# Projection units in another order, their weights split without the second rounded copy, weight sums started elsewhere, norm sums copied by ScalarE

## The chip, the cores and the metric

The kernel runs on one core of a Trainium2 chip. A core has a matrix engine (TensorE, PE in the rows; PEld is its weight load), VectorE (DVE), ScalarE (ACT), GpSimd (POOL) and a queue that issues DMAs (SP). The metric is the device time of one execution in microseconds: 2397.79 us is the median of three runs of the kernel before (2397.59 to 2398.81).

## What is computed

One streaming step of a one-layer encoder trunk on 1024 prompt frames and 64 sample frames (1088 tokens, 1024 channels, all float32):

```
h = x + 1/2 * SwiGLU_1(RMSNorm(x))
z = RMSNorm(h) @ w_in            # columns [u_ssm 512 | q 512 | k 512 | v 512]
y_ssm = GLU(S5(u_ssm))           # diagonal complex state, scan over time; gelu; y * sigmoid(y @ w_glu + b)
y_att = DiffAttn(q, k, v)        # 4 heads
h = h + concat(y_ssm, y_att) @ w_out
h = h + CrossAttn(RMSNorm(h), RMSNorm(mem))      # weights w_cq, w_ck, w_cv, w_co
x = h + 1/2 * SwiGLU_2(RMSNorm(h))
y = RMSNorm(x)
```

It also returns k and v of the new tokens, the memory's k and v and the last S5 states. The change lies almost wholly in the second line, the input projection, and in what runs beside it.

## The kernel before

**Float32 by three products.** Each operand of a matmul is split into a rounded high part and the rest. `mm3` (L172) then makes three matmuls per tile, high by high, high by low and low by high. For the weights, `load_w` (L166) loads 128x512 pieces (tiles `wr`, four buffers) and `w_split` (L155) splits each into `wh` and `wl` (seven buffers each). There are two ways to split. The staged one (`split_into`, L147 to L154) has ScalarE write the high part twice, once as `wh` into SBUF (L152) and once into a PSUM bank `q` (L153), and VectorE subtract `q` from the raw weights (L154). The tag `q` has one buffer. The other way (L162, L163) has ScalarE write `wh` only and VectorE subtract `wh`.

**The projection stage.** `w_in` is done in 16 units of 128 output columns: u0 to u3, then k, q and v of each head. One unit loads two pieces of weights and runs 72 matmuls into three PSUM banks (`unit`, `units`, L179 to L193); VectorE then multiplies the banks by the token norms `rb` (L1387 for u units, L203 for the others). PSUM has seven such banks beside `q`. The rows of 1088 tokens come from one pool of 36 buffers.

**The norms.** FFN1 delivers eight rows of `h` (`mix_row`). For each, `Stats.add` squares it on ScalarE (L259) and adds it to a sum on GpSimd (L260, seven adds after the first row). When all are in, `Stats.rstd` reduces the sum over channels by matmuls with ones (L269), VectorE forms the roots (L220 to L232), PE transposes them (L138) and ScalarE writes `rb`. TensorE has the matmuls with ones right behind the 72 matmuls of the first unit, u0.

**S5.** Each u unit starts one chain `s5_main`: store u, load it regrouped, matmuls (L1291), scans on VectorE (`scaled` and `scan`, L1262 to L1272), the scan over blocks in a small tile `gs` (from L1305, with its first writes L1305 and L1308), loads, the y products on TensorE (L1340, L1341) and gelu on ScalarE (L1342), stores (L1345).

**Weight sums.** Later square layers use sums and differences of four 512x512 quarters of a weight. `weight_sums` makes them on GpSimd: for each k of four, four tiles are loaded (L478, two DMAs each), four additions run on each (L482 to L485) and the tile is stored (L486). 16 tiles and 64 additions a weight. The tiles are of the tag `ws`, four buffers, which `gs` shares. Before, `w_out` is summed beside FFN1 and `w_co`, then `w_cq`, from head 2 of the projection stage on.

**The order.** The order of instructions on each engine, and of DMAs on SP, is set once at build time by a scheduler that simulates the program; on the chip each engine and each queue then goes through its own list in order, and an instruction that waits holds up all that stand behind it on its engine. `bg` holds generators that are advanced (`pump_all`) between units.

**Normed.finish** is called twice in FFN2; it reduces norms as `Stats.rstd` does, and two small copies (L602, L603) take the result out of PSUM.

Of the kernel before, what the change touches and what calls it, by code (L numbers as in the profile page):

```python
# [17 lines left out]
P = 128  # L18
# [3 lines left out]
NS = 64  # L22
# [9 lines left out]
NC = NT // TS  # L32
NCP = NP // TS
NPAIR = 16
SUMS_AT = 2
S_CHS = ((0, 360), (360, 720), (720, 1088))
NROWS = 36
BIG = 3.0e38
# [31 lines left out]
def tile_hymba_step(ctx: ExitStack, tc: tile.TileContext, a, o):  # L70
# [24 lines left out]
    def row(shape=(P, NT), dt=F32):  # L95
        return rows.tile(list(shape), dt, tag="r", name=nm("r"))
# [13 lines left out]
    bg = deque()  # L110
# [10 lines left out]
    def pump_all():  # L121

        for g in list(bg):
            try:
                next(g)
            except StopIteration:
                bg.remove(g)
# [38 lines left out]
    def load_w(src, staged=True):  # L166

        parts = [w_split(w_raw(src[:, k:k + 4]), staged) for k in range(0, src.shape[1], 4)]
        return [(hi[:, k], lo[:, k]) for hi, lo in parts for k in range(4)]
# [9 lines left out]
    def units(wsrcs, xs, mid=None, at=None, chs=CHS):  # L179


        n = len(xs)
        ws = [load_w(src) for src in wsrcs]
        ps_ = [[bank() for _ in range(3)] for _ in ws]
        for k0, k1 in ((0, at or n), (at or n, n)):
            for w, p in zip(ws, ps_):
                mm3(p, ((*w[k], *xs[k]) for k in range(k0, k1)), n, chs, k0)
            if mid and k0 == 0:
                mid()
        return ps_  # L190
# [279 lines left out]
    def weight_sums(n, w, swap=False):  # L470

        i11, i21, i12, i22 = (1, 0, 3, 2) if swap else (0, 1, 2, 3)
        for k in range(4):
            ts = [half([P, 4, P]) for _ in range(4)]
            for c, t in enumerate(ts):
                for h in range(2):
                    wj = w[(4 * h + k) * P:(4 * h + k + 1) * P].rearrange("p (h c n) -> p h c n", h=2, c=4)
                    load(out=t[:, 2 * h:2 * h + 2], in_=wj[:, :, c])  # L478
            yield
            for c, t in enumerate(ts):  # L480
                a11, a21, a12, a22 = (t[:, i] for i in (i11, i21, i12, i22))
                G.tensor_tensor(out=a22, in0=a21, in1=a22, op=ALU.add)  # L482
                G.tensor_tensor(out=a21, in0=a11, in1=a21, op=ALU.subtract)
                G.tensor_tensor(out=a11, in0=a22, in1=a11, op=ALU.subtract)
                G.tensor_tensor(out=a12, in0=a12, in1=a11, op=ALU.subtract)  # L485
                store(out=sums_d[n, k, c], in_=t)  # L486
# [85 lines left out]
    class Normed:  # L572
# [22 lines left out]
        def finish(self, c):  # L595
            ssq = small([P, 5], "hq")
            V.memset(ssq, 1.0)
            p = bank()
            for t, (t0, n) in enumerate(HTILES):
                T.matmul(p[:n, 4 * t:4 * t + 4], self.acc[:, c, t0:t0 + n], ones[:, 0:4], start=True, stop=True)  # L600
            n = HT - 512
            V.tensor_copy(ssq[:, 0:4], p[:, 0:16].rearrange("p (t n) -> p t n", n=4)[:, :, 0])  # L602
            V.tensor_copy(ssq[:n, 4:5], p[:n, 16:17])  # L603
            if self.rb is None:
                self.rb = row()
            yield from half_rstd(ssq, self.rb, c)
# [667 lines left out]
    def s5_main(f, u):  # L1274
        js = slice(4 * f, 4 * f + 4)

        store(out=u_d[f], in_=u)
        w1 = row([P, 4, 2, P])
        load(out=w1, in_=w1_d[f])
        u8 = row([P, 8, NC])  # L1280
        for s in range(TS):
            load(out=u8[16 * s:16 * s + 16], in_=u_d[f, :, s].rearrange("(g h) c -> h g c", h=16))
        yield
        yield

        p = [bank() for _ in range(3)]
        for i in range(8):
            q, j = i // 4, i % 4
            e = p[i // 3][:, (i % 3) * NC:(i % 3 + 1) * NC]
            for r in range(2):  # L1290
                T.matmul(e[64 * r:64 * r + 64], w1[:, j, q, 64 * r:64 * r + 64], u8[:, 2 * j + r],  # L1291
                         start=True, stop=True)
        x = row([P, 8, NC])
        three(x, p)
        yield

        r_ = row()
        tu = r_[:, 0:544], r_[:, 544:1088]
        for k in (1, 2, 4):
            scan(x, k, tu, f, (apr, api, apn))  # L1300
            yield

        gs = half([P, 152]).rearrange("p (r n) -> p r n", n=19)
        xe = x.rearrange("p r (s i) -> p r s i", i=8)[:, :, :, 7]
        V.memset(gs[:, :, 0:1], 0.0)  # L1305
        V.tensor_copy(gs[:, :, 1:17], xe[:, :, 0:16])
        for q in range(2):
            V.tensor_copy(gs[:, 4 * q:4 * q + 4, 17], cf[:, 6 + q, js])  # L1308
        V.tensor_tensor(out=gs[:, :, 18:19], in0=xe[:, :, 16:17],
                        in1=scaled(tu, f, (apr, api, apn), 7, 1, gs[:, :, 17:18], 1)[:, :, :, 0], op=ALU.add)  # L1310
        for k in (1, 2, 4, 8):
            scan(gs[:, :, 1:17], k, tu, f, wide)
        for b in range(2):
            for q in range(2):
                V.tensor_copy(s_fin[:, b, q, js], gs[:, 4 * q:4 * q + 4, 16 + 2 * b])
        V.tensor_copy(gs[:, :, 16:17], gs[:, :, 17:18])
        yield
        s_ = row([P, 8, NC])
        sv, xv = (z.rearrange("p r (s i) -> p r s i", i=8) for z in (s_, x))
        V.tensor_copy(sv[:, :, :, 0], gs[:, :, 0:17])  # L1320
        scaled((sv[:, :, :, 1:8], row()), f, (apr, api, apn), 0, 7, gs[:, :, 0:17], 17)
        V.tensor_tensor(out=sv[:, :, :, 1:8], in0=xv[:, :, :, 0:7], in1=sv[:, :, :, 1:8], op=ALU.add)
        yield
        xs_ = row([P, 8, NC])
        for i in range(2):
            for q in range(2):
                load(out=xs_[64 * i:64 * i + 64, q::2], in_=s_[64 * q:64 * q + 64, 4 * i:4 * i + 4])
        yield
        m, rk = row([P, 8, P]), row([P, 8, P])
        load(out=m, in_=m_d[f])  # L1330
        load(out=rk, in_=rk_d[f].rearrange("p g s h -> p g (s h)"))
        yield
        yield

        y8 = s_
        for b, n in ((0, 3), (1, 3), (2, 2)):
            p = bank()
            for g in range(n):
                q = p[:, g * NC:(g + 1) * NC]
                T.matmul(q, m[:, 3 * b + g], u8[:, 3 * b + g], start=True, stop=False)  # L1340
                T.matmul(q, rk[:, 3 * b + g], xs_[:, 3 * b + g], start=False, stop=True)  # L1341
            A.activation(y8[:, 3 * b:3 * b + n].rearrange("p g n -> p (g n)"), p[:, :n * NC], AF.Gelu_apprx_tanh)  # L1342
            yield
        for s in range(TS):
            store(out=ys_d[f, :, s].rearrange("(g h) c -> h g c", h=16), in_=y8[16 * s:16 * s + 16])  # L1345
        yield
        y = row([P, TS, NC])
        load(out=y, in_=ys_d[f])
        yT[f] = y
# [27 lines left out]
    def in_unit(c, by_step=False):  # L1377

        chs = S_CHS if by_step else CHS
        p = unit(wi[:, :, c * P:(c + 1) * P], xs, pump_all, chs)  # L1380
        if rb[0] is None:
            rb[0] = st1.rstd()
        if not by_step:
            return times(p, rb[0])
        z = row([P, TS, NC])
        for pc, (c0, c1) in zip(p, chs):
            V.tensor_tensor(out=z.rearrange("p s c -> p c s")[:, c0 // TS:c1 // TS],  # L1387
                            in0=pc[:, :c1 - c0].rearrange("p (c s) -> p c s", s=TS),
                            in1=rb[0][:, c0:c1].rearrange("p (c s) -> p c s", s=TS), op=ALU.mult)
        return z  # L1390
# [35 lines left out]
        G.tensor_scalar(out=wide[2], in0=wide[1], scalar1=-1.0, scalar2=None, op0=ALU.mult)  # L1426

    wide_powers()
    bg.append(weight_sums(0, a["w_out"][0]))
    for f in range(4):  # L1430
        u = in_unit(f, True)
        pump_all()
        bg.append(s5_main(f, u))
    kT, qT, vt, vsr = [], [], [], row([NS, 4, P])
    for hd in range(4):
        if hd == SUMS_AT:
            bg.append(chain(weight_sums(2, a["w_co"][0]), weight_sums(1, a["w_cq"][0], True)))
        k = in_unit(8 + hd)
        pump_all()
        kT.append(k)  # L1440
        bg.append(to_tokens(k, row([P, 8, P]), row([NS, P]), "new_attn_k_prompt", "attn_k_sample", hd))
        qT.append(in_unit(4 + hd))
        pump_all()
        v = in_unit(12 + hd)
        pump_all()
        vt.append(row([P, 8, P]))
        bg.append(to_tokens(v, vt[hd], vsr[:, hd], "new_attn_v_prompt", "attn_v_sample", hd))
    pump(1000)
    s5_final_states()

# [230 lines left out]
    for f in range(4):  # L1681
# [7 lines left out]
        z = row()  # L1689
# [372 lines left out]
```

## Time and profile before

| | |
|---|---|
| median of 3 runs | 2397.79 us |
| the profiled execution | 2398.3 us |
| its span | 2396.5 us |
| mean granted TensorE clock | 0.982 of full |
| PE busy | 2262.8 us (94%) |
| DVE busy | 1644.8 us (69%) |
| ACT busy | 1290.2 us (54%) |
| POOL busy | 1101.7 us (46%) |

The projection stage runs from about 798 to 1046 us of the span, FFN1 before it, attention behind it. TensorE is the busiest engine in nearly every part, so a time that can change is one in which TensorE has nothing to do or runs below full clock; the window and gap views below show where these are.

### The profile page before, as it was taken

To read this page: it belongs to the slowest core of one execution; us is meant where nothing else is said; L and a number is where in the kernel's file an instruction comes from. 1 tells how busy PE (TensorE), PEld (TensorE's weight loads), DVE (VectorE), ACT (ScalarE), POOL (GpSimd) and SP (SyncE) were. 2 spreads that over 40 slices of the span, in tenths; PEclk is the share of its full clock that TensorE was granted. 3 is DMA by queue.
4 is the path that set the end of the run, shared out by engine and by line. 5 is a ranking of instruction groups with operands and counts; after the bars stand their busy time and mean duration, and the time that the engine had idled before them with its cause. 6 is when DMAs were issued, how large, how long until landed. Compare 5 with 4: busy or idle time off the path is not lost. (4 is left out here: it accounts for less than half of the span.)

```text
span 2396.5 us, 45406 instructions
## 1 busy us (share of the span) xinstructions
PE 2262.8 (94%) x16914; PEld 2197.2 (92%) x16914; DVE 1644.8 (69%) x3318; ACT 1290.2 (54%) x2506; POOL 1101.7 (46%) x968
## 2 busy tenths in 40 slices
PE   6999999999998997998999999898999999998998
PEld 5999999999998997997799999798899999998988
DVE  6757434358898596248977888787654455479897
ACT  6554544546544521247866767676555545464543
POOL 1566776754167414425511400043776666644350
PEclk8999999999999998999999999999999999999999
DMA  6232444453424557854346530252232222262212
GB/s 207 79 116 79 119 112 121 113 180 137 146 80 146 170 148 203 255 175 121 117 134 200 184 124 28 85 162 89 86 99 77 81 69 77 82 233 83 106 47 93
DMA packets 325033, 297.26 MB, mean 124 GB/s; under 512 B 39454, under 2 KB 268875, under 8 KB 324811
## 3 DMA queue, kind: packets, MB, share of 16 engines
q1 hardware_dynamic: 324720, 294.33, 39.0%
q8 instruction: 133, 2.18, 0.4%
q14 instruction: 90, 0.73, 0.1%
q10 hardware_dynamic: 90, 0.02, 0.0%
HBM read 208.53 MB, written 81.17 MB: 121 GB/s over the span
## 5 line engine op out<-in xcount | busy, mean ns | idle before, releaser
L176 PE MATMUL b<-r,wh 128*128 128x272 f32 (+4 forms) x9600 | 1684.8, 296 | 55.1 <-DVE r L780 24.9
L176 PEld LDWEIGHTS b<-r,wh 128*128 128x128 f32 x9600 | 1417.5, 190 | 72.1 <-DVE r L780 30.5
L176 PE MATMUL b<-r,wl 128*128 128x272 f32 (+4 forms) x4800 | 1054.6, 295 | 17.3 <-DVE wl L154 17.1
L176 PEld LDWEIGHTS b<-r,wl 128*128 128x128 f32 x4800 | 784.4, 190 | 22.0 <-DVE wl L154 21.8
L652 DVE TENSOR_TENSOR r<-b,r 128x272 f32<-128x272 f32 x440 | 172.1, 434 | 237.0 <-PE b L176 216.7
L154 DVE TENSOR_TENSOR wl<-wr,q 128x512 fp32r<-128x512 f32 x272 | 185.4, 682 | 150.0 <-issue 77.9
L153 ACT CAST q<-wr 128x512 fp32r<-128x512 f32 x272 | 161.4, 593 | 229.7 <-DVE wl L154 221.0
L152 ACT CAST wh<-wr 128x512 fp32r<-128x512 f32 x272 | 167.9, 622 | 196.8 <-PE b L176 191.4
L455 DVE TENSOR_TENSOR r<-r,r 128x544 fp32r<-128x544 f32 x224 | 201.4, 919 | 22.9 <-ACT r L454 22.4
L154 DVE TENSOR_TENSOR wl<-ws,q 128x512 fp32r<-128x512 f32 x182 | 123.9, 681 | 100.3 <-PE b L176 53.7
L152 ACT CAST wh<-ws 128x512 fp32r<-128x512 f32 x182 | 112.7, 620 | 137.6 <-PE b L176 110.0
L593 POOL TENSOR_TENSOR r<-r,r 128x544 f32<-128x544 f32 x28 | 43.6, 1558 | 282.2 <-ACT r L592 281.5
L153 ACT CAST q<-ws 128x512 fp32r<-128x512 f32 x182 | 107.8, 592 | 113.4 <-DVE wl L154 98.2
L454 ACT CAST r<-r 128x544 fp32r<-128x544 f32 x224 | 144.6, 653 | 10.0 <-DMA r<-hid_d 8.4
L780 DVE SCALAR_TENSOR_TENSOR r<-b,r 128x272 f32<-128x272 f32 (+4 forms) x328 | 132.0, 438 | 19.4 <-PE b L176 18.4
L153 ACT CAST q<-r 128x512 fp32r<-128x512 f32 x122 | 72.4, 593 | 126.4 <-DVE wl L154 126.3
L702 POOL TENSOR_TENSOR r<-r,r 128x544 f32<-128x544 f32 x44 | 62.4, 1419 | 161.3 <-DVE r L652 135.8
L672 POOL TENSOR_TENSOR ws<-wr,wr 128x512 f32<-128x512 f32 x44 | 60.4, 1372 | 156.9 <-DMA wr<-w_ffn_gu 126.4
L715 POOL TENSOR_TENSOR r<-r,r 128x1088 f32<-128x1088 f32 x44 | 111.7, 2540 | 8.1 <-ACT r L714 8.1
L138 PE MATMUL b<-ident,r 128*128 128x128 f32 (+4 forms) x649 | 92.5, 280 | 23.9 <-DMA r<-x_prompt 10.6
L138 PEld LDWEIGHTS b<-ident,r 128*128 128x128 f32 (+4 forms) x649 | 74.6, 144 | 34.9 <-DMA r<-x_prompt 10.6
L154 DVE TENSOR_TENSOR wl<-r,q 128x512 fp32r<-128x512 f32 x122 | 83.1, 681 | 29.3 <-ACT q L153 25.0
(348 smaller groups left out, 2978.7 us busy)
## 6 DMA issues: line engine op xcount, KB each, us to landing
wr<-w_ffn_gu SPq DMA_DIRECT2D x194, 256.0 KB, 3.0
hid_d<-r SPq DMA_DIRECT2D x44, 544.0 KB, 2.9
r<-hid_d SPq DMA_DIRECT2D x44, 544.0 KB, 6.5
h_d<-r SPq DMA_DIRECT2D x48, 272.0 KB, 2.1
r<-h_d SPq DMA_DIRECT2D x48, 272.0 KB, 4.3
r<-w_ffn_d SPq DMA_DIRECT2D x24, 512.0 KB, 6.7
sums_d<-ws SPq DMA_DIRECT2D x48, 256.0 KB, 3.5
wr<-w_in SPq DMA_DIRECT2D x32, 256.0 KB, 2.9
```

The costliest lines, as they stand in the source:

```text
L138: T.transpose(out, in_, ident[:n, :n])
L152: A.copy(hi, x)
L153: A.copy(r, x)
L154: V.tensor_tensor(out=lo, in0=x, in1=r.bitcast(F32), op=ALU.subtract)
L176: T.matmul(pc[:, :c1 - c0], w, x[:, c0:c1], start=(first + i == 0 and q == 0), stop=(first + i == n - 1 and q == 2))
L454: A.copy(r[:, 0], v)
L455: V.tensor_tensor(out=r[:, 1], in0=v, in1=r[:, 0].bitcast(F32), op=ALU.subtract)
L652: V.tensor_tensor(out=oc, in0=pc, in1=tc_, op=ALU.add)
L672: G.tensor_tensor(out=s1, in0=r[2], in1=r[3], op=ALU.add)
L702: G.tensor_tensor(out=gate[:, T2], in0=gate[:, T2], in1=up[:, T2], op=ALU.add)
L715: G.tensor_tensor(out=up, in0=up, in1=gate, op=ALU.mult)
L780: V.scalar_tensor_tensor(out=hc_, in0=pc, scalar=0.5, in1=hc_, op0=ALU.mult, op1=ALU.add)
```

## The change

Five things are changed. The 16 units run in another order, u2 and u3 between the first k, q and v. The weights of all units (`w_in` and `w_glu`, 36 pieces) are split the second way. The sums of `w_co` start directly behind those of `w_out`, and `w_cq` alone is begun at the 12th unit. In `Normed.finish` ScalarE makes the two copies. The rest of the diff is the loop written anew.

```diff
-SUMS_AT = 2
+SUMS_AT = 11
+UNITS = "u0 u1 k0 u2 q0 u3 v0 k1 q1 v1 k2 q2 v2 k3 q3 v3".split()
...
-        ws = [load_w(src) for src in wsrcs]
+        ws = [load_w(src, False) for src in wsrcs]
...
-            V.tensor_copy(ssq[:, 0:4], p[:, 0:16].rearrange("p (t n) -> p t n", n=4)[:, :, 0])
-            V.tensor_copy(ssq[:n, 4:5], p[:n, 16:17])
+            A.copy(ssq[:, 0:4], p[:, 0:16].rearrange("p (t n) -> p t n", n=4)[:, :, 0])
+            A.copy(ssq[:n, 4:5], p[:n, 16:17])
...
-    bg.append(weight_sums(0, a["w_out"][0]))
-    for f in range(4):
-        u = in_unit(f, True)
+    bg.append(chain(weight_sums(0, a["w_out"][0]), weight_sums(2, a["w_co"][0])))
+    kT, qT, vt, vsr = [], [], [], row([NS, 4, P])
+
+    def make(kind, n):
+
+        c = {"u": 0, "q": 4, "k": 8, "v": 12}[kind] + n
+        z = in_unit(c, kind == "u")
         pump_all()
-        bg.append(s5_main(f, u))
...
-        if hd == SUMS_AT:
-            bg.append(chain(weight_sums(2, a["w_co"][0]), weight_sums(1, a["w_cq"][0], True)))
-        k = in_unit(8 + hd)
-        pump_all()
...
+    for i, name in enumerate(UNITS):
+        if i == SUMS_AT:
+            bg.append(weight_sums(1, a["w_cq"][0], True))
+        make(name[0], int(name[1]))
```

Lines of the changed kernel are one higher than before up to the stage's loop, so L260 is L261 there, L154 is L155, L163 is L164 and L1342 is L1343.

The first place is GpSimd at the end of FFN1. Before, the last additions of `w_out` are followed by the seven adds of the norms with nothing between but the first of the wide powers of S5 (r_9709). r_9482 is the sum of the norms, the ws are tiles of weight sums:

```order
L485 TENSOR_TENSOR ws_10077<-ws_10077 128x128
L485 TENSOR_TENSOR ws_10078<-ws_10078 128x128
L260 TENSOR_TENSOR r_9482<-r_9482,r_9513 128x1088
L260 TENSOR_TENSOR r_9482<-r_9482,r_9545 128x1088
L260 TENSOR_TENSOR r_9482<-r_9482,r_9577 128x1088
L260 TENSOR_TENSOR r_9482<-r_9482,r_9609 128x1088
L260 TENSOR_TENSOR r_9482<-r_9482,r_9641 128x1088
L260 TENSOR_TENSOR r_9482<-r_9482,r_9673 128x1088
L1415 COPY r_9709<-apow_r 128x16
L1416 COPY r_9709<-api 128x16
L1421 TENSOR_TENSOR r_9709<-r_9709 128x16
L260 TENSOR_TENSOR r_9482<-r_9482,r_9705 128x1088
```

Now 22 additions of `w_co` stand ahead of the first of these adds, and 17 between the first and the seventh; this is the stretch around the first three.

```order
L484 TENSOR_TENSOR ws_10259<-ws_10259 128x128
L261 TENSOR_TENSOR r_9482<-r_9482,r_9513 128x1088
L485 TENSOR_TENSOR ws_10259<-ws_10259 128x128
L483 TENSOR_TENSOR ws_10260<-ws_10260 128x128
L261 TENSOR_TENSOR r_9482<-r_9482,r_9545 128x1088
L486 TENSOR_TENSOR ws_10259<-ws_10259 128x128
L483 TENSOR_TENSOR ws_10261<-ws_10261 128x128
L484 TENSOR_TENSOR ws_10260<-ws_10260 128x128
L261 TENSOR_TENSOR r_9482<-r_9482,r_9577 128x1088
```

The adds themselves are the same seven; what moved is the work of `w_co`, from the middle of the stage to between them.

The second place is ScalarE in the middle of the stage, at the first gelus of S5. Before, a copy into the bank `q` stands ahead of the gelus (L1342):

```order
L153 CAST q_11605<-wr_11601 128x512
L1342 ACTIVATE r_10560<-b_11005 128x408
L152 CAST wh_11603<-wr_11601 128x512
L153 CAST q_11613<-wr_11609 128x512
L1342 ACTIVATE r_10560<-b_11110 128x272
L1342 ACTIVATE r_10765<-b_11116 128x408
```

Now no copy into `q` of this stage is left, and the gelus (L1343) stand between the high parts alone:

```order
L163 CAST wh_11611<-wr_11609 128x512
L1343 ACTIVATE r_10652<-b_11142 128x272
L1343 ACTIVATE r_10823<-b_11148 128x408
L163 CAST wh_11617<-wr_11615 128x512
L1343 ACTIVATE r_10823<-b_11231 128x408
```

What is gone from the list is what made the gelus wait for VectorE's subtraction.

The third place is VectorE behind the first unit. Now the first write of the third `gs` tile (ws_11027) stands ahead of the multiplications that empty the banks of u1 (b_9925 to b_9927); before, the four such writes stood in FFN1.

```order
L1306 MEMSET ws_11027 128x8
L1309 COPY ws_11027<-cf 128x4 x2
L1388 TENSOR_TENSOR r_10044<-b_9925,r_9861 128x45x8
L1388 TENSOR_TENSOR r_10044<-b_9926,r_9861 128x45x8
L1388 TENSOR_TENSOR r_10044<-b_9927,r_9861 128x46x8
```

The tile is the same buffer as a tile of `w_co`, so this write is behind the landing of that tile's store.

## Rows read from the trace of the kernel before

**Rows 1.** Busy time by window, us: TensorE's clock (PEclk) is the share of full.

```profile
800.00:820.00 20.00, 17.40 (x110) 16.51 (x109) 9.90 (x18) 7.29 (x12) 12.64 (x25) 1.00 0.41 139
820.00:840.00 20.00, 20.00 (x140) 19.58 (x140) 5.29 (x8) 5.38 (x10) 0.00 (x0) 1.00 0.56 143
...
900.00:920.00 20.00, 13.61 (x79) 12.80 (x77) 20.00 (x50) 3.15 (x6) 11.64 (x15) 0.91 0.65 183
920.00:940.00 20.00, 18.79 (x97) 18.47 (x98) 14.02 (x33) 3.75 (x8) 7.80 (x10) 0.74 0.68 184
940.00:960.00 20.00, 14.52 (x80) 14.31 (x79) 7.22 (x10) 4.25 (x9) 8.83 (x16) 0.83 0.88 259
```

**Rows 2.** Timeline of PE: start, duration, then the idle time before.

```profile
905.50 2.00 PE L138 MATMUL b<-ident,r 128*128 128x128 f32 x9 [1.86 <-DVE r L203]
920.61 0.82 PE L1340 MATMUL b<-r,r 128*128 128x136 f32 x2 [5.14 <-ACT r L1342]
924.31 0.97 PE L176 MATMUL b<-r,wh 128*128 128x364 f32 x2 [0.60 <-ACT r L1342]
947.94 0.82 PE L1340 MATMUL b<-r,r 128*128 128x136 f32 x2 [5.48 <-DMA ws<-w_co]
```

**Rows 3.** Timeline of ACT and DVE around those gaps.

```profile
919.64 0.59 ACT L153 CAST q<-wr 128x512 fp32r<-128x512 f32 x1 [4.88 <-DVE wl L154]
920.16 0.39 ACT L1342 ACTIVATE r<-b 128x272 f32<-128x272 f32 x1
...
918.93 0.68 DVE L154 TENSOR_TENSOR wl<-wr,q 128x512 fp32r<-128x512 f32 x1
...
942.71 0.96 DVE L1263 TENSOR_TENSOR r<-ws,apn 128x476 f32<-128x476 f32 x1 [6.73 <-DMA ws<-w_co]
```

**Rows 4.** Timeline of PE, then of POOL, at the end of FFN1.

```profile
805.89 0.66 PE L176 MATMUL b<-r,wl 128*128 128x360 f32 x3
807.48 2.42 PE L269 MATMUL b<-ones,r 128*128 128x128 f32 x18 [0.94 <-POOL r L260]
...
782.35 2.71 POOL L260 TENSOR_TENSOR r<-r,r 128x1088 f32<-128x1088 f32 x1 [14.68 <-ACT r L259]
786.51 16.92 POOL L260 TENSOR_TENSOR r<-r,r 128x1088 f32<-128x1088 f32 x5 [1.45 <-ACT r L259]
803.37 1.27 POOL L1415 COPY r<-apow_r 128x16 f32<-128x16 f32 x1
804.91 2.52 POOL L260 TENSOR_TENSOR r<-r,r 128x1088 f32<-128x1088 f32 x1
```

**Rows 5.** SP: a stretch of the timeline, a DMA group (last: us to landing), one line.

```profile
765.60 3.63 SPq L486 DMA_DIRECT2D sums_d<-ws  x4
...
sums_d<-ws SPq DMA_DIRECT2D x48, 256.0 KB, 3.5
...
L478 SPq DMA_DIRECT2D ws<-w_co x32: 540/604/875, 873.8 to 972.8; - x32
DMA to landing us min/median/max: 2.5/2.9/5.0
```

**Rows 6.** Timeline of POOL in FFN1, then groups by line: busy us, mean ns.

```profile
739.16 0.45 POOL L485 TENSOR_TENSOR ws<-ws 128x128 f32<-128x128 f32 x1
749.00 0.94 POOL L482 TENSOR_TENSOR ws<-ws 128x128 f32<-128x128 f32 x1
...
L482 POOL TENSOR_TENSOR ws<-ws 128x128 f32<-128x128 f32 x48 | 30.2, 631 | 154.8 <-DVE r L1265 63.9 <-DMA ws<-w_co 53.5 <-issue 16.2
L485 POOL TENSOR_TENSOR ws<-ws 128x128 f32<-128x128 f32 x48 | 27.1, 569 | 1.7
```

**Rows 7.** Timeline of DVE at the other way to split, alone and beside POOL.

```profile
1250.43 0.68 DVE L163 TENSOR_TENSOR wl<-wr,wh 128x512 fp32r<-128x512 f32 x1
1352.35 5.67 DVE L163 TENSOR_TENSOR wl<-wr,wh 128x512 fp32r<-128x512 f32 x4
```

**Rows 8.** Timeline of DVE at one of the two small copies.

```profile
1643.50 0.15 DVE L602 COPY hq<-b 128x4 f32<-128x4 f32 x1
```

More of the change, by code (lines that the diff above doesn't have):

```diff
@@ L1428, in tile_hymba_step @@
     wide_powers()
-    bg.append(weight_sums(0, a["w_out"][0]))
-    for f in range(4):
-        u = in_unit(f, True)
-        pump_all()
-        bg.append(s5_main(f, u))
-    kT, qT, vt, vsr = [], [], [], row([NS, 4, P])
-    for hd in range(4):
-        if hd == SUMS_AT:
-            bg.append(chain(weight_sums(2, a["w_co"][0]), weight_sums(1, a["w_cq"][0], True)))
-        k = in_unit(8 + hd)
-        pump_all()
[L1440 to L1447, printed above, removed]
+    bg.append(chain(weight_sums(0, a["w_out"][0]), weight_sums(2, a["w_co"][0])))
[3 more added lines that the diff above has]
+        z = in_unit(c, kind == "u")
+        pump_all()
+        if kind == "u":
+            bg.append(s5_main(n, z))
+        elif kind == "q":
+            qT.append(z)
+        elif kind == "k":
+            kT.append(z)
+            bg.append(to_tokens(z, row([P, 8, P]), row([NS, P]), "new_attn_k_prompt", "attn_k_sample", n))
+        else:
+            vt.append(row([P, 8, P]))
+            bg.append(to_tokens(z, vt[n], vsr[:, n], "new_attn_v_prompt", "attn_v_sample", n))
+    for i, name in enumerate(UNITS):
+        if i == SUMS_AT:
+            bg.append(weight_sums(1, a["w_cq"][0], True))
+        make(name[0], int(name[1]))
     pump(1000)
```

## The prediction

> **What bounds the kernel now.** I read the windows first. TensorE is busy in nearly all of the projection stage, so time can be had only where it idles or runs below full clock. From 900 to 960 it is busy 13.61, 18.79 and 14.52 of 20 us, at 0.91, 0.74 and 0.83 of full clock [rows 1]. VectorE is busy for all of 900 to 920, and so is the bottleneck there; from 820 to 840 it has 5.29 us of work and GpSimd none [rows 1]. The four S5 chains, started one behind the other by u0 to u3, make that crowd.
>
> Then the gaps of TensorE in these 60 us: 1.86, 5.14, 0.60 and 5.48, in all 13.1 us [rows 2]. The clock after them costs more: the busy times by what is missing of full clock are 13.61 x 0.09 + 18.79 x 0.26 + 14.52 x 0.17 = 8.6 us [rows 1]. What can be won is 13.1 + 8.6 = 21.7 us.
>
> What releases the gaps: the y products (L1340) of the 5.14 us gap wait for a bank that a gelu empties; the gelu, at 920.16, stands behind ScalarE's copy into `q`, which started at 919.64 after 4.88 us of idling for VectorE's subtraction; that one had come at 918.93 [rows 3]. So a full VectorE holds ScalarE through the one bank `q`, and ScalarE holds TensorE. The 5.48 us gap carries a DMA's name. VectorE itself idled 6.73 us until 942.71 [rows 3], for a row of the pool whose last reader is a store of y, and the release of the y products stood behind that.
>
> Last, the end of FFN1. TensorE has finished u0 at 805.89 + 0.66 = 806.55 and starts the matmuls with ones at 807.48, 0.94 us late, released by GpSimd's last add of norms (804.91 + 2.52 = 807.43) [rows 4]. All later work of the stage stands behind these matmuls. GpSimd is thus already, barely, the last to arrive there, and the change puts work into its queue at just this place.
>
> **The change part by part.** *Sums of `w_co` beside the norms (a loss).* GpSimd idled 14.68 us before the first add at 782.35 [rows 4], and the scheduler has filled this hole, and more, with 22 additions. When does the 22nd end? The last stores of `w_out` are issued from 765.60 to 769.23 [rows 5]. The first `w_co` tile takes two loads, issued in 2 x 0.60 us, that land 2.9 us after [rows 5], about 773; two tiles' additions (8 x 0.45 us [rows 6], partly waiting for loads) go to about 777. The store of the first tile is queued on SP behind loads of `w_in` that wait for VectorE's splits, as before, and so goes out near 776.5; it lands 3.5 us later [rows 5], at 780.0. Only then may the tile's buffer be loaded again: two loads with a store between, out at 781.4, landed at 784.3. Six additions remain, about 2.9 us: the first add of norms starts near 787.2, in place of 782.35.
>
> From there to the end of the seventh: the adds themselves take 2.71 + 16.92 + 2.52 = 22.15 us [rows 4]; 17 additions at 0.60 us (between the lines' means of 0.57 and 0.63 [rows 6]) are 10.2 us; the copies and products of the wide powers between them are 1.9 us, 1.27 of it one copy [rows 4]. 787.2 + 22.15 + 10.2 + 1.9 = 821.5, so the matmuls with ones start 14.0 us later. Nothing covers this: TensorE has no other work ahead of them in its list. The bounds: additions at 0.45 us and no delay of the first add give 782.35 + 22.15 + 7.7 + 1.9 = 814.1, 6.7 us late. Additions at 0.94 us [rows 6], the first add 3 us later for them and the adds 2 us longer in all give 832, 25 us late. I take 14, since GpSimd is beside a busy VectorE until about 805 and free of it afterwards.
>
> A gap of this size lowers the clock. Behind the 5.14 us gap the clock in 920 to 940 lost 18.79 x 0.26 = 4.9 us, behind the 5.48 us gap 2.5 us [rows 1]. The new gap is followed by more stops (matmuls with ones, roots, transposes) at which TensorE works little. I take 4, bounds 2 and 7. Together +18.
>
> *The split without `q` (a gain).* 36 copies into `q` go from ScalarE, and with them the wait that held the gelu: the 5.14 and the 0.60 us gap lose their cause. VectorE's own instruction stays, at the same 0.68 us when alone [rows 7].
>
> Beside GpSimd the row shows something else: four such splits in 5.67 us, 1.4 each, at 1352.35 [rows 7]. The Trainium skill says why (SBUF — State Buffer, section "SBUF: two separate sides"): an instruction of VectorE with two SBUF inputs and a GpSimd instruction that reads SBUF exclude each other for their whole length, since both need a shared pair of ports. The staged subtraction had one input in PSUM; the new one has two in SBUF, so by the rule the change adds contention exactly where `w_co` is summed, and the row agrees with it. By it the 17 additions would be nearer 0.94 than 0.60 us, and the sum nearer the rival of contention below.
>
> *The order of units (a gain).* One S5 chain now starts with every second or third unit, so the scans spread over twice the matmuls and VectorE should no longer be full from 900 to 920. With that, the 1.86 us gap and the wait for a row lose their cause too. But a list in order brings stops of its own, and rows of the pool are now waited for at other places. I count 70% of the 21.7 us: −15; bounds −21.7 (all gone) and −6 (only the gap of the gelu and its clock, less new stops).
>
> *The first writes of `gs` (a small loss).* Each needs the buffer of a `w_co` tile, freed when its store lands; the third stands ahead of the emptying of u1's banks on VectorE. That tile's additions come at the end of GpSimd's list, near 836, and its store behind the eight loads of u0's regrouping on SP, near 837; landing at 837 + 3.5 = 840.5. The matmuls of u1 end near 842 if u0's norms are 14 us late, so it is hidden by this same delay: I take 1, bounds 0 and 4.
>
> *`w_cq` later and the two copies.* `w_cq` has no reader in the stage. The two copies take VectorE 0.15 us each, twice [rows 8]; nobody waits for them within microseconds. Together 0, bounds −2 and +2, with the small shifts in FFN2's lists.
>
> The sum: 14 + 4 − 15 + 1 = +4 against the profiled execution of 2398.3, hence 2402.3. That execution lies 0.5 above the median of the runs, so about 2401.5 there; I say 2401.
>
> **The rivals.** *The gain without the loss.* GpSimd fits the additions into its hole, the first add is on time, the delay is the lower bound of 6.7 us with 2 us of clock, and all 21.7 us come back: −13, 2385. For it speaks that the hole was 14.68 us and 22 additions at 0.45 us are 9.9; against it that the second round of tiles must wait for a store to land, and that the order puts a further 17 additions behind.
>
> *Contention (the other side).* One mechanism: GpSimd's additions between the adds run at 0.94 us, at the place where VectorE has the row multiplications, FFN1's sums and the new splits. The matmuls with ones start 25 us late, with 5 us of clock, and 13 come back: +17, 2415. It decides from the point at which the delay and its clock exceed the 22 us that can be won. For it: from 690 to 767 GpSimd has rows such as that of 0.94 at 749.00 [rows 6]; against it: VectorE has little to do from 805 on.
>
> *The loss without the gain.* The lists of the changed kernel make TensorE stop as often at other places (rows of the pool, y products): +18 − 6 = +12, 2410. For it: the old gaps too were in a list that a simulation found free of stops; against it: two of four gaps came through `q`, which is gone.
>
> **How the numbers follow.** The sum as it stands has 0.42, the gain without the loss 0.27, contention 0.18, the loss without the gain 0.13. A measurement of this kernel can tell 0.2%, 4.8 us. Below 2393 lie the second case and a sliver of the first: faster 0.28. Above 2402.6 lie the third, the fourth and a fifth of the first: slower 0.39. The rest, 0.33, is within. The first case's own range is 2394 to 2410; to hold eight in ten I go from 2384 to 2416, which takes in the lower rival and the point of contention.
>
> **What would show it.** Right: in the window 800 to 820 TensorE is busy several us less than 17.40, with one idle time of 10 us or more ahead of the matmuls with ones, released by the add of norms; GpSimd is at work without a hole from 773 to 835; the clock is below 1.00 for some 8 us behind; from 900 to 960 VectorE is no longer at 20.00, no y product waits for a gelu over 1 us, and the clock is 1.00. The prediction is wrong if the matmuls with ones start before 813, or if idle times of over 10 us in sum remain among the later units.

## The result, and the profile after

The changed kernel takes 2411.03 us (median of four runs, 2408.98 to 2411.68) against 2398.3 us for the kernel before on the same chip: 1.0051 times as long, 95% interval 1.0039 to 1.0063, so 12.7 us slower. The forecast was 2401, and the time lies inside its range, near its upper end. The span of the profiled execution grew by 12.9 us, from 2396.5 to 2409.4.

Two marks in the trace say where. The matmuls with ones start at 821.47 instead of 807.48 [rows 4], 14.0 us later. The gated linear unit, behind the projection units, starts its first cast at 1062.6 instead of 1049.2, 13.4 us later. So all the time is lost ahead of the first of these marks, and the units between them give back no more than the clock takes.

TensorE's stops in the changed kernel, by its timeline (start, duration, and in brackets the idle time before and its releaser):

```profile
821.47 4.40 PE L270 MATMUL b<-ones,r 128*128 128x128 f32 x18 [13.62 <-POOL r L261]
...
928.43 3.89 PE L1292 MATMUL b<-r,r 128*64 128x136 f32 x32 [8.23 <-DMA r<-u_d]
...
990.52 0.82 PE L1341 MATMUL b<-r,r 128*128 128x136 f32 x2 [5.42 <-ACT r L1343]
```

The four gaps of before [rows 2] are gone. In their place stand the stop for the norms, and two that did not exist before: 8.23 us for a load of u, and 5.42 us for a gelu. The busy times by window (columns as in [rows 1], which the first two and the next three answer):

```profile
800.00:820.00 20.00, 7.84 (x47) 7.45 (x46) 10.32 (x6) 4.57 (x5) 20.00 (x21) 0.82 0.60 199
820.00:840.00 20.00, 16.15 (x77) 15.08 (x78) 5.39 (x17) 2.12 (x5) 16.59 (x45) 0.67 0.70 218
...
900.00:920.00 20.00, 20.00 (x129) 20.00 (x127) 19.83 (x34) 3.65 (x5) 9.29 (x8) 1.00 0.52 166
920.00:940.00 20.00, 11.77 (x85) 11.19 (x85) 8.51 (x39) 3.40 (x7) 3.95 (x9) 0.83 0.83 231
940.00:960.00 20.00, 20.00 (x136) 20.00 (x135) 19.90 (x26) 4.06 (x8) 12.04 (x16) 1.00 0.79 215
...
980.00:1000.00 20.00, 14.58 (x85) 14.25 (x83) 2.68 (x5) 3.86 (x8) 6.27 (x15) 0.91 0.94 270
```

GpSimd (the fifth of the pairs) is busy for all of 800 to 820, where it was for 12.64, and TensorE (the first) for 7.84 instead of 17.40. The clock stays low for some time behind the stop; finer windows show that it is at half, the lower of the two levels, when the matmuls with ones begin, and 0.73 on the average of 830 to 836:

```profile
818.00:824.00 6.00, 2.54 (x12) 2.54 (x13) 0.16 (x1) 0.00 (x0) 6.00 (x13) 0.50 0.59 176
824.00:830.00 6.00, 3.61 (x16) 2.81 (x15) 2.28 (x9) 0.75 (x2) 4.00 (x13) 0.50 0.43 149
830.00:836.00 6.00, 6.00 (x29) 5.73 (x28) 2.24 (x3) 0.74 (x3) 5.48 (x18) 0.73 0.96 303
```

From 836 to 842 it is 1.00. Busy time by what is missing of full clock gives 2.54 x 0.50 + 3.61 x 0.50 + 6.00 x 0.27 = 4.7 us.

On GpSimd, whose rows answer [rows 4], the adds of norms (L261) stand between additions of `w_co` (L483 to L486):

```profile
773.72 0.46 POOL L483 TENSOR_TENSOR ws<-ws 128x128 f32<-128x128 f32 x1 [4.46 <-DMA ws<-w_co]
...
789.37 3.61 POOL L261 TENSOR_TENSOR r<-r,r 128x1088 f32<-128x1088 f32 x1
792.93 1.51 POOL L485 TENSOR_TENSOR ws<-ws 128x128 f32<-128x128 f32 x1
...
817.37 0.45 POOL L484 TENSOR_TENSOR ws<-ws 128x128 f32<-128x128 f32 x1
...
818.95 2.46 POOL L261 TENSOR_TENSOR r<-r,r 128x1088 f32<-128x1088 f32 x1
```

The first add starts at 789.37 and not 782.35; the seventh ends at 821.41. Beside VectorE an addition takes up to 1.51 us, later 0.45.

The stop of 8.23 us is explained on SP. Its timeline, with the store of u3 (L1278) and the eight loads that bring it back regrouped (L1283):

```profile
904.39 0.54 SPq L1278 DMA_DIRECT2D u_d<-r  x1
...
907.60 1.21 SPq L479 DMA_DIRECT2D ws<-w_cq  x2
915.38 0.33 SPq L487 DMA_DIRECT2D sums_d<-ws  x1
...
917.46 0.55 SPq L479 DMA_DIRECT2D ws<-w_cq  x1
918.10 2.65 SPq L1328 DMA_DIRECT2D r<-r  x4
920.80 0.60 SPq L1280 DMA_DIRECT2D r<-w_d  x1
921.45 3.92 SPq L1283 DMA_DIRECT2D r<-u_d  x8
```

From 908.81 to 915.38 SP stands at L487, the store of a summed tile of `w_cq`; the loads of u3 are behind it. That store waits for GpSimd's last addition on the tile (L486), and the tile's first addition is this:

```profile
908.81 4.41 POOL L483 TENSOR_TENSOR ws<-ws 128x128 f32<-128x128 f32 x1 [11.00 <-DMA ws<-w_cq]
913.30 0.83 POOL L484 TENSOR_TENSOR ws<-ws 128x128 f32<-128x128 f32 x1
...
914.82 0.54 POOL L486 TENSOR_TENSOR ws<-ws 128x128 f32<-128x128 f32 x1
```

An instruction of 0.45 us took 4.41. Over the same time VectorE went without a break through the scans and a split, all with two inputs in SBUF:

```profile
908.82 1.15 DVE L1266 TENSOR_TENSOR r<-r,r 128x952 f32<-128x952 f32 x1
909.88 0.72 DVE L1266 TENSOR_TENSOR r<-r 128x544 f32<-128x544 f32 x1
910.52 0.69 DVE L164 TENSOR_TENSOR wl<-wr,wh 128x512 fp32r<-128x512 f32 x1
911.12 1.15 DVE L1323 TENSOR_TENSOR r<-r,r 128x952 f32<-128x952 f32 x1
912.18 0.72 DVE L1273 TENSOR_TENSOR r<-r,r 128x544 f32<-128x544 f32 x1
```

So an addition whose result nobody reads for more than 400 us is late beside VectorE and holds up a store; the store holds up the loads behind it in SP's list, and these hold TensorE. That VectorE is what delays the addition is read from the two timelines side by side; no run takes it away alone.

The stop of 5.42 us is on ScalarE (these rows answer [rows 3]). The old wait for `q` is gone from the stage's own weights, but the scheduler put the copy of the next stage's weights (`w_out`) ahead of the gelu, and this one waited for its load. SP (first row) issued that load at 985.84, after a wait of 0.6 us for the landing of the store of a weight sum, since the load goes into a tile of the tag `ws` too:

```profile
985.84 0.34 SPq L508 DMA_DIRECT2D ws<-w_out  x1
...
989.43 0.59 ACT L154 CAST q<-ws 128x512 fp32r<-128x512 f32 x1 [12.50 <-DMA ws<-w_out]
989.96 0.50 ACT L1343 ACTIVATE r<-b 128x408 f32<-128x408 f32 x1
```

### The profile page after: what moved, and what is told of

Read it like the earlier page. It is cut to its first block, busy times and chain, and to the rows that moved or that the text cites. A ratio compares the mean times of both kernels' runs of the same rounds, so it can differ in the third digit from the quotient of the medians.

```text
span 2409.4 us, 45346 instructions
## 1 busy us (share of the span) xinstructions
PE 2262.0 (94%) x16914; PEld 2196.2 (91%) x16914; DVE 1658.6 (69%) x3314; ACT 1271.3 (53%) x2474; POOL 1106.1 (46%) x968
## 5 line engine op out<-in xcount | busy, mean ns | idle before, releaser
L177 PE MATMUL b<-r,wh 128*128 128x272 f32 (+5 forms) x9600 | 1680.1, 296 | 55.1 <-DVE r L781 27.4
L155 DVE TENSOR_TENSOR wl<-wr,q 128x512 fp32r<-128x512 f32 x236 | 160.8, 681 | 101.4 <-issue 52.1
L154 ACT CAST q<-wr 128x512 fp32r<-128x512 f32 x236 | 140.2, 594 | 169.3 <-DVE wl L155 166.7
L456 DVE TENSOR_TENSOR r<-r,r 128x544 fp32r<-128x544 f32 x224 | 203.3, 927 | 23.8 <-ACT r L455 22.4
L153 ACT CAST wh<-wr 128x512 fp32r<-128x512 f32 x236 | 146.2, 622 | 105.5 <-PE b L177 99.1
L155 DVE TENSOR_TENSOR wl<-ws,q 128x512 fp32r<-128x512 f32 x182 | 124.0, 681 | 99.9 <-PE b L177 54.0
L154 ACT CAST q<-ws 128x512 fp32r<-128x512 f32 x182 | 107.9, 593 | 115.8 <-DVE wl L155 95.7
L154 ACT CAST q<-r 128x512 fp32r<-128x512 f32 x122 | 72.4, 594 | 125.3 <-DVE wl L155 125.2
L163 ACT CAST wh<-wr 128x512 fp32r<-128x512 f32 x68 | 41.5, 619 | 175.9 <-PE b L177 139.8
```

What stands on the lines that cost most here:

```text
L153: A.copy(hi, x)
L154: A.copy(r, x)
L155: V.tensor_tensor(out=lo, in0=x, in1=r.bitcast(F32), op=ALU.subtract)
L177: T.matmul(pc[:, :c1 - c0], w, x[:, c0:c1], start=(first + i == 0 and q == 0), stop=(first + i == n - 1 and q == 2))
L456: V.tensor_tensor(out=r[:, 1], in0=v, in1=r[:, 0].bitcast(F32), op=ALU.subtract)
```

## The experiments

All kernels, with the starts of the matmuls with ones and of the gated linear unit's first cast, and the span, each from the kernel's one profiled execution. Ratios are those of the times to the kernel before on the same chip, with 95% intervals. Executions of one kernel lie up to 12 us apart (e3: 2387.55 to 2399.97), so a difference of a few us between two marks of different kernels decides nothing.

| kernel | ratio | ones | linear unit | span |
|---|---|---|---|---|
| before | | 807.5 | 1049.2 | 2396.5 |
| after | 1.0051 (1.0039 to 1.0063) | 821.5 | 1062.6 | 2409.4 |
| e1 | 1.0107 (1.0092 to 1.0123) | 816.0 | 1062.8 | 2418.9 |
| e2 | 1.0064 (1.0044 to 1.0083) | 819.7 | 1064.6 | 2413.7 |
| e3 | 0.9988 (0.9977 to 0.9999) | 807.1 | 1051.7 | 2395.6 |
| e4 | 1.0080 (1.0065 to 1.0095) | 816.4 | 1068.1 | 2412.1 |
| e5 | 1.0064 (1.0048 to 1.0079) | 807.0 | 1054.7 | 2410.9 |
| e6 | 1.0037 (1.0019 to 1.0054) | 809.3 | 1064.8 | 2410.7 |
| e7 | 0.9901 (0.9882 to 0.9920) | 807.4 | 1028.1 | 2376.7 |
| e8 | 1.0001 (0.9990 to 1.0012) | 806.2 | 1049.2 | 2400.4 |
| e9 | 1.0008 (0.9997 to 1.0019) | 809.2 | 1049.5 | 2395.0 |
| e10 | 1.0013 (0.9998 to 1.0028) | 808.1 | 1049.6 | 2395.7 |
| e11 | 1.0046 (1.0031 to 1.0061) | 816.7 | 1063.0 | 2409.3 |
| e12 | 1.0054 (1.0041 to 1.0068) | 806.6 | 1027.1 | 2406.9 |

**e1: the split alone.** The kernel before with one edit:

```diff
-        ws = [load_w(src) for src in wsrcs]
+        ws = [load_w(src, False) for src in wsrcs]
```

> The kernel before with one edit: the weights of all units are split without the copy into q. Theory (the loss of the change is the sums of w_co between the adds of norms, and the copy into q was what held the gelus): the matmuls with ones start at 807 to 809 as before, the gaps of 5.14 and 0.60 us before the y products go with some 5 us of clock, so 5 to 11 us faster than before: 2387 to 2393. Rival (the new split, with two SBUF inputs, loses as much by contention with GpSimd as it gains): 2396 to 2402.

Measured 2420.65 us, the slowest of all: the theory fell, the part that was booked as a gain is a loss. The matmuls with ones come 8.5 us late although GpSimd has no work of `w_co` there. GpSimd's adds of norms, and VectorE's new splits beside them, in the timelines of GpSimd and of VectorE:

```profile
786.99 5.95 POOL L260 TENSOR_TENSOR r<-r,r 128x1088 f32<-128x1088 f32 x2 [0.49 <-ACT r L259]
```

```profile
787.58 5.90 DVE L163 TENSOR_TENSOR wl<-wr,wh 128x512 fp32r<-128x512 f32 x2
```

Two splits that take 0.68 each alone [rows 7] and two adds of 2.5 us each [rows 4] make 2 x 0.68 + 2 x 2.5 = 6.4 us one after the other; they took from 786.99 to 793.48, 6.5 us, side by side. They go in turns. The Trainium skill states this exclusion, which the prediction weighed (SBUF — State Buffer, section "SBUF: two separate sides"). The trace agrees with it here: 5.90 us for 1.36 us of work. While VectorE is in its splits it does not empty FFN1's banks, and TensorE stops in FFN1 for 3.32 us. A second stop of 2.50 us follows at 814.18, and the matmuls with ones then come without a gap:

```profile
793.99 0.97 PE L176 MATMUL b<-r,wh 128*128 128x362 f32 x2 [3.32 <-DVE r L780]
...
816.02 3.15 PE L269 MATMUL b<-ones,r 128*128 128x128 f32 x18
```

So here TensorE itself is late; GpSimd's last add of norms is over at 812.98. Of the 22.4 us of the span the rest is later: stops of 6.19 us at 928.95 and 6.64 us at 1046.17, and 8 us in FFN2.

**e2: the sums alone.** The kernel before with `w_co` directly behind `w_out`, and `w_cq` alone at head 2:

```diff
-    bg.append(weight_sums(0, a["w_out"][0]))
+    bg.append(chain(weight_sums(0, a["w_out"][0]), weight_sums(2, a["w_co"][0])))
...
-            bg.append(chain(weight_sums(2, a["w_co"][0]), weight_sums(1, a["w_cq"][0], True)))
+            bg.append(weight_sums(1, a["w_cq"][0], True))
```

> The kernel before with one edit: the sums of w_co start right behind those of w_out, w_cq stays at head 2. Theory: the matmuls with ones start at 818 to 823 in place of 807.5, with 5 to 7 us of clock behind; the later stops stay about as they were: 2410 to 2420. Rival (the late start is taken back by a stage that is bound by something else, VectorE, until 930): VectorE catches up while TensorE stands, the gaps of 900 to 960 shrink as the start is later, and the time is 2398 to 2405.

Measured 2412.21 us, as the theory has it. Of the later stops, those between 900 and 970 are no shorter than before: 1.37, 6.61, 0.60 and 7.80 us. TensorE's first stop:

```profile
819.74 4.40 PE L269 MATMUL b<-ones,r 128*128 128x128 f32 x18 [11.91 <-POOL r L260]
```

With the old split and the old order the start is 12.2 us late; of the 14.0 us the sums alone make nearly all. The 8.5 us of e1 do not add to them: in the changed kernel e1's two stops of TensorE are not there, and u0 is finished at 807.84.

**e3: the order alone.** The new order of units, the old split, `w_co` and `w_cq` together from the eleventh unit on:

```diff
-SUMS_AT = 2
+SUMS_AT = 10
+UNITS = "u0 u1 k0 u2 q0 u3 v0 k1 q1 v1 k2 q2 v2 k3 q3 v3".split()
...
+        if i == SUMS_AT:
+            bg.append(chain(weight_sums(2, a["w_co"][0]), weight_sums(1, a["w_cq"][0], True)))
```

> The kernel before with one edit: the units in the new order (w_co and w_cq chained and begun at the unit k2, as before at head 2; copy into q kept). Theory (the new stops of the changed kernel at 920 and 985 come through the queue of SP from the sums of w_cq, not from the order): start as before, VectorE no longer full, gaps between 900 and 1000 under 8 us in sum: 2385 to 2395. Rival (the order itself makes TensorE wait for the regrouped u and for y): gaps of 10 us or more remain, 2396 to 2406.

Measured 2395.02 us, 0.1% below before. The order alone is no gain of 10 us: the start is on time, yet the stage is as long as before. Gaps of 14.3 us in sum remain between 900 and 1000, as the rival has it; the time lies between the two forecasts. The largest stop is the one of the changed kernel, with the old split, and again the store of a summed tile, here of `w_co`, stands ahead of the loads of u3 on SP:

```profile
910.26 3.89 PE L1292 MATMUL b<-r,r 128*64 128x136 f32 x32 [7.88 <-DMA r<-u_d]
```

**e4: the changed kernel with the sums taken out of the norms**, and started as in e3:

```diff
-SUMS_AT = 11
+SUMS_AT = 10
...
-    bg.append(chain(weight_sums(0, a["w_out"][0]), weight_sums(2, a["w_co"][0])))
+    bg.append(weight_sums(0, a["w_out"][0]))
...
-            bg.append(weight_sums(1, a["w_cq"][0], True))
+            bg.append(chain(weight_sums(2, a["w_co"][0]), weight_sums(1, a["w_cq"][0], True)))
```

> The changed kernel with one edit taken back: w_co and w_cq are summed where they were, chained and begun at the unit k2; new order, split without q and ScalarE copies stay. Theory: the matmuls with ones start at 807 to 809, 20 us of the loss go, and the stops at 920 and 985 go too since both came through sums in the queue of SP: 2377 to 2386. Rival (the sums cost only the late start, the two later stops belong to the order): 2389 to 2394.

Measured 2413.87 us: both wrong. The start is still 9.0 us late, with two stops in FFN1 of 3.37 and 2.41 us as in e1, and the stop for u comes again:

```profile
922.28 3.81 PE L1292 MATMUL b<-r,r 128*64 128x136 f32 x32 [8.98 <-DMA r<-u_d]
```

**e5: the new split from the fifth unit on**, that is, not beside FFN1's norms; else the kernel before:

```diff
+    done = [0]
...
-        ws = [load_w(src) for src in wsrcs]
+        ws = [load_w(src, done[0] < 4) for src in wsrcs]
+        done[0] += 1
```

> The kernel before, with the split without q only from the fifth unit on (u0 to u3 keep the copy into q, so no split with two SBUF inputs runs beside the adds of norms on GpSimd). Theory (the split alone lost at the end of FFN1 because splits and adds of norms exclude each other: two splits took 5.90 us there, 0.64 each elsewhere): the matmuls with ones start at 807 to 809 again, in place of 816, and the time is 2388 to 2400. Rival (the loss of the split alone came from its later stops and from FFN2's lists): the start is early again, but the time stays above 2408.

Measured 2414.33 us, so the rival is right: the start is on time, 807.0, and the lateness of e1's start came from these first units, but they make only about 9 of e1's 23.8 us. The end is late all the same, with new stops, the first long one for a load of S5. On SP this load is issued at 913.50; ahead of it the store of a summed tile of `w_co` waits 6.9 us for GpSimd, until 906.32:

```profile
918.68 0.79 PE L1343 MATMUL b<-r,r 128*128 128x136 f32 x2 [5.73 <-DMA r<-m_d]
```

**e6: e4 with this late split**, so the new order, the sums at the eleventh unit, no late start:

> The changed kernel with the sums of w_co and w_cq back at the unit k2 and the copy into q kept for the first four units. Theory: start at 807 to 809, the new order's stop of some 8 us before the matmuls on u3 stays, the stops for gelus go: 2385 to 2396, 15 us or more below the changed kernel. Rival (each list brings its own stops, whatever is taken away): 2397 to 2410.

Measured 2409.5 us, in the rival's range, with the same stop of 8.99 us for u, one of 9.16 at 962 and one of 5.00 at 1047. Three builds start the norms on time and none of them reaches the linear unit earlier than before: 1051.7, 1054.7 and 1064.8. What e3, e5 and e6 share are the sums of `w_co` and `w_cq` in the stage, which are left out next.

**e7: e6 without the sums of `w_co` and `w_cq`.** They are not made, and the layers that use them read those of `w_out`. The results of these layers are then not theirs, but all their loads and matmuls stay the same in number and size:

```diff
-                      in_=sums_d[self.number, k, :, :, i].rearrange("c p n -> p c n"))
+                      in_=sums_d[0, k, :, :, i].rearrange("c p n -> p c n"))
...
-        if i == SUMS_AT:
-            bg.append(chain(weight_sums(2, a["w_co"][0]), weight_sums(1, a["w_cq"][0], True)))
```

> The kernel e6 without any sums of w_co and w_cq: the two layers that use them read the sums of w_out instead, so all later loads and matmuls are the same in number and size, and only the 32 tiles' loads, additions and stores are left out. Theory (the stop before the matmuls on u3 is SP's: its loads of the regrouped u stand behind loads and stores of sums that wait for GpSimd and VectorE): the stop falls from 8 to under 4 us and the time is 6 to 14 us below e6. Rival (the stop is the order's own, since the loads stand behind those of u1's or u2's states, which wait for VectorE): it stays at 6 us or more, and the time within 4 us of e6.

Measured 2376.42 us, 33 us below e6, and the linear unit starts at 1028.1 instead of 1064.8. The same place on SP, first in e6, then in e7: the store of u3 (L1281) and the loads that bring it back (L1286), with what stands between:

```profile
887.38 0.54 SPq L1281 DMA_DIRECT2D u_d<-r  x1
888.02 0.38 SPq L146 DMA_DIRECT2D wr<-w_in  x1
890.70 1.21 SPq L482 DMA_DIRECT2D ws<-w_co  x2
898.50 0.33 SPq L490 DMA_DIRECT2D sums_d<-ws  x1
...
904.55 4.40 SPq L1286 DMA_DIRECT2D r<-u_d  x8
```

```profile
883.58 0.32 SPq L1281 DMA_DIRECT2D u_d<-r  x1
884.09 1.52 SPq L146 DMA_DIRECT2D wr<-w_in  x1
...
895.93 3.76 SPq L1286 DMA_DIRECT2D r<-u_d  x8
```

TensorE waits 1.92 us there in e7, 8.99 in e6. Not all of the lag is the sums': the loads go out 17.2 us behind the store in e6 and still 12.4 in e7. TensorE's stops of over 0.5 us from 820 to 1060, ahead of the linear unit, add up to 27.3 us in e6 and to 1.9 in e7. Of the windows (840 to 960, first e6, then e7) the third column, VectorE, is to be read against the first, TensorE:

```profile
840.00:960.00 120.00, 103.93 (x698) 102.13 (x696) 95.26 (x235) 20.66 (x37) 36.14 (x40) 0.95 0.55 156
```

```profile
840.00:960.00 120.00, 118.08 (x810) 116.76 (x808) 102.08 (x255) 24.14 (x44) 0.00 (x0) 1.00 0.58 159
```

Without the sums VectorE has even more to do in this stretch, and TensorE runs through it at full clock. So a full VectorE by itself does not stop TensorE; with the sums beside it TensorE stops.

**e8: the two copies of `Normed.finish` by ScalarE**, alone.

> The kernel before with one edit: ScalarE makes the two small copies of Normed.finish. Theory (nobody waits for them within microseconds): 2396 to 2400. Rival (FFN2's lists shift by the edit and with them its stops): 3 us or more to either side.

Measured 2398.84 us, ratio 1.0001: nothing, as forecast.

**e9, e10, e11: the sums begun in attention** (`bg.append(chain(...))` at the attention loop's second step), in the kernel before, in e6 and in the changed kernel.

> The kernel before with the sums of w_cq and w_co begun in the attention loop (two score steps in), in place of head 2 of the projection stage; all else as before. Theory (the sums are what makes the stage stop, wherever in it they stand, through the queue of SP and the four ws buffers): the 5.48 us gap and some of the others go, the stage ends 5 to 12 us earlier and attention loses less than half of that: 2387 to 2395. Rival (the work only moves its stops into attention, where VectorE is busy 35 to 38 of 40 us): 2397 to 2406.

> Units in the new order, copy into q kept for the first four units only, ScalarE copies, and the sums of w_cq and w_co begun in the attention loop. Theory: the stage as in the kernel without these sums (norms at 807, the GLU's first cast near 1030 in place of 1049), less some stops where the first sums slip into its end, and a few us of loss in attention: 2378 to 2389, faster than both kernels. Rival (the sums cost in attention what they cost in the stage): 2396 to 2408.

> The changed kernel with one edit: the sums of w_co and w_cq are begun in the attention loop; order, split without q for all units and ScalarE copies stay. Theory: the matmuls with ones start at 815 to 817 (the split beside the adds of norms, as when it stood alone), the stops at 920 and 985 go, so 12 to 24 us below the changed kernel: 2387 to 2399. Rival (the order's stops stay): 2403 or more.

Measured 2399.42, 2402.4 and 2408.37 us, each in its rival's range and none in its theory's. They decide nothing on the place of the sums: the scheduler started them in the projection stage all the same, as soon as tiles were free (in e9 and e10 the additions of these sums are over by 1050), and e10 and e11 have the stop for u again, 8.16 and 8.29 us. They repeat that the early split costs the start (e11: 816.7, e9 and e10: 809.2 and 808.1).

**e12: the sums kept out of the stage by a dependence.** As e10, with a copy out of the linear unit's last result into each tile of a sum's first quarter, so that no load of the sums can start earlier:

```diff
+                if gate[0] is not None and k == 0:
+                    for i in (0, 2):
+                        G.tensor_copy(t[:, i, 0:1], gate[0])
...
+    gate[0] = const([P, 1], "gate")
+    G.tensor_copy(gate[0], z[:, 0:1])
```

> The new order of units, the second rounded copy kept for the first four units and left out from the fifth, the norm sums copied by ScalarE, and the whole sums of w_cq and w_co made behind the gated linear unit: one GpSimd copy out of the unit's last result into each tile of the first quarter of each sum (32 copies of one column, a few us of GpSimd in all) keeps the loads of those sums from starting before. So the projection stage holds no weight sum but those of w_out. Theory (the stage's stops are those of SyncE's list and of the sums' buffers): the stage goes as in e7_no_later_sums, the store of u and its regrouping loads follow each other within about 17 us, the statistics start at about 807 and the gated linear unit's first cast stands at 1028 to 1035 instead of 1049.2 before and 1062.6 in the changed kernel; attention, where GpSimd and SyncE then hold 128 additions and 96 DMAs more, gives some 5 to 12 us of it back. Time 2380 to 2392, faster than the kernel before by 6 to 18 us. Rival (the sums cost wherever they stand as much as in the projection stage, some 20 to 33 us by e7 against before and against e6): the gated linear unit as early, but the end at 2396 to 2408. Third case: the projection stage isn't shorter (first cast behind 1045), then the stops there were not those of the sums.

Measured 2411.64 us. The first half is as the theory says: the linear unit starts at 1027.1, 22 us earlier than before and 1 us from e7. The second half is the rival's, and a little beyond: the end comes 30.2 us behind e7. The windows of e7, then of e12:

```profile
1000.00:1100.00 100.00, 91.39 (x535) 82.80 (x534) 64.06 (x156) 56.28 (x109) 32.07 (x46) 0.95 0.36 112
1100.00:1200.00 100.00, 94.26 (x658) 80.16 (x657) 95.05 (x348) 82.03 (x197) 46.72 (x65) 1.00 0.38 115
```

```profile
1000.00:1100.00 100.00, 87.43 (x474) 79.07 (x473) 58.64 (x127) 50.71 (x98) 45.15 (x79) 0.88 0.45 142
1100.00:1200.00 100.00, 78.93 (x501) 66.92 (x501) 83.47 (x265) 64.01 (x147) 83.55 (x155) 0.92 0.64 199
```

TensorE is busy 19.3 us less in these 200, and runs at a lower clock: busy time by what is missing of full clock is 87.43 x 0.12 + 78.93 x 0.08 = 16.8 us in e12 and 91.39 x 0.05 = 4.6 in e7. 19.3 + 12.2 = 31.5 us, close to the 30.2. GpSimd has 49.9 us more. What is seen there is like what is seen in the stage. Of SP's three largest waits two are for the sums (us in total, times, longest, from 1025 to 1200), and TensorE's longest stop is for a load of the key cache that SP issued at 1161.28, between loads and stores of `w_co`:

```profile
SPq L495 <- POOL ws L494: 34.6, 15, 7.0
...
SPq L487 <- DMA sums_d<-ws: 20.1, 15, 3.3
```

```profile
1163.69 1.94 PE L139 MATMUL b<-ident,r 128*128 128x128 f32 x8 [6.02 <-DMA r<-cache_attn_k]
```

So these two sums cost over 30 us in both places where they were put: 33 us in the projection stage (e6 against e7), 35 us in attention (e12 against e7, on different chips). No complete kernel that was run beats before by more than e3's 0.1%.

## Why the prediction was right and where it failed

The time is inside the range, but the range was drawn to hold the other cases too: the first case's own range of 2394 to 2410 ends just short of 2411.03. And its own sign of being wrong came true, "if idle times of over 10 us in sum remain among the later units": 8.23 + 5.42 = 13.6 us remain. Of its parts the loss was right and the gain was not. (2402.3 less 0.5 is 2401.8, where the prediction has 2401.5; nothing hangs on it.)

**The late start: right, 14 us forecast and 14.0 measured** (821.5 and 821.47), and e2 shows that the sums make it. Inside the step the errors cancel, which is luck: the first add came 2.2 us later than worked out and the 17 additions took 12.6 us, 0.74 each, instead of 10.2; the seven adds took 19.6 instead of 22.15 us and the copies 0.8 instead of 1.9.

**Its clock: 4 forecast, 4.7 measured.**

**The first writes of `gs`: 1 forecast, 0 measured.** The third of these writes was expected at 840.5 and came at 842.31; the emptying of u1's banks began at 843.65, released by TensorE. The late start hides it, as the step said.

**The two copies: 0 forecast, 0 measured** (e8).

**The gain in the units: the step that failed.** "I count 70% of the 21.7 us: −15". The four gaps did go. But the two new stops are 8.23 + 5.42 = 13.6 us, and their clock is 11.77 x 0.17 + 14.58 x 0.09 = 3.3 us by the windows above. Of 21.7 us, 4.8 are won. (One execution gives the 21.7 only to some 3 us: e8, where nothing in this stage was edited, has 24.7 by the same working.) By the marks it is 13.4 − 14.0 − 4.7 = −5.3, the same. With −5 for −15 the prediction's own sum is 14 + 4.7 − 5 + 0 = +14, against the 12.7 us measured. The rival that had this as its content, "the loss without the gain", +12 and 2410, was the right one; it was given 0.13.

**Why it failed** lies in the reading of the first part: "a full VectorE holds ScalarE through the one bank `q`". The row was right, but it named the wait that came last, and e5 and e6, in which the copies into `q` are gone from the fifth unit on, stop as often. The second reading, that spread scans would free VectorE, fails too: it is busy for 19.32, 19.69 and 19.83 of 20 us from 860 to 920 after the change, and in e7 it is as full and TensorE stops once, for 1.92 us. What e3, e5, e6 and the changed kernel have in common are the sums, in SP's list ahead of loads that TensorE needs, and e7 takes 33 us away with them. A clue stood in the rows: one of TensorE's four waits, of 5.48 us, and VectorE's of 6.73 us carried the name of a load of `w_co` [rows 2, 3], and the prediction set the name aside for a row of the pool.

**The split was costed with the wrong sign.** "VectorE's own instruction stays, at the same 0.68 us when alone". By the new split alone e1 is 23.8 us slower, and e5, which keeps the old split beside GpSimd's adds of norms, is still 15.0 slower. The prediction did see the exclusion, and booked it only on the additions of `w_co`; that splits and adds of norms also hold each other, and with them FFN1's banks and TensorE, was missed. In the changed kernel it costs little: TensorE finishes u0 at 807.84, and the start is 14.0 us late with both, 12.2 with the sums alone (e2).

**Still open.** Which part of the sums costs the 30 us, the place in SP's list, GpSimd's time beside VectorE, the tiles or the DMAs themselves, no run separates; the chain shown is one stop of several. Nor was the old order run without the sums, so what the new order would be worth in a kernel without them is not known. In e1 and e5 about 8 us of the loss arise in FFN2 alone (against before, e1 is 14.2 us late at FFN2's first matmuls with ones, L600, and 22.4 at the end), and why was not tried.

## What to carry to other kernels

Work that nobody needs for long is not free only because its engine is idle: its loads and stores sit in an ordered list, and here the loads behind them inherited their waits. Before booking the end of a stop as a gain, ask what the next wait in the same list is, and test by leaving the background work out altogether, which here told more in one run than the rearrangements before it. And an instruction that changes an input in PSUM for one in SBUF is to be timed beside GpSimd, not alone.

## What the runs showed of the hardware

A GpSimd addition of 128x128 that takes 0.45 us alone took 4.41 us while VectorE ran an unbroken row of instructions with two SBUF inputs, none of them longer than 1.15 us. The next six additions took 0.54 to 0.94 us, although VectorE's row went on. It goes the other way too: two splits of 0.68 us took 5.90 beside two adds of norms, and pairs of splits in the changed kernel 1.81 to 3.86. So the price of such a pair isn't one factor, and it can be longer than any single instruction of the other engine.

After 13.62 us without work TensorE's granted clock was 0.50, the lower level, stayed there while TensorE had little to do (2.54 and 3.61 of 6 us), and was full again behind 836. In e12, with stops of up to 6.02 us scattered over 200 us, its mean was 0.88 and 0.92 in the two halves: many short stops cost more through the clock (12.2 us more than in e7) than the three long ones of the changed kernel (4.7 + 3.3 us).
